# The delta rule's turns placed by a schedule clock among the projections, and its memory handed first to attention's inputs

## The chip, the core and the metric

The kernel runs on one core of a Trainium2 chip. The metric is the device time of one execution in microseconds (us). A core has TensorE (PE in the profile; its weight loads are PEld), VectorE (DVE), ScalarE (ACT), GpSimd (POOL) and SyncE (SP, which here issues nearly all DMAs). Each engine works through its own list of instructions, and semaphores make one wait for another.

## What is computed

One layer of 2048 tokens and width 1024, with two groups of four heads that read the same normalised input:

```python
h = rmsnorm(x, norm_gain)
proj = einsum('btd,dc->btc', h, w_in)          # 4104 columns
dn_q, dn_k, dn_v, dn_z, dn_b, dn_a, df_q, df_k, df_v, df_z = split(proj)
o_dn = gated_deltanet_group(...)   # conv of width 4, SiLU, delta rule with decay, norm(o) * silu(z)
o_df = diff_attention_group(...)   # two causal softmax maps a head, A1 - lam * A2, norm * silu(z)
x = x + einsum('btc,cd->btd', concatenate([o_dn, o_df]), w_out)
```

The delta rule, head by head, is a recurrence over chunks: a triangular system is solved for each chunk, and a state of 128x128 goes from chunk to chunk.

## The kernel before

Matmul inputs are split into a high and a low part of type fp32r, and a product is three matmuls (high by high, high by low, low by high). The kernel is written as generators, each of which gives the hand back (`yield`) after a small piece of work, called a turn or a step here. The order of the program is the order in which the generators are called; the framework then schedules each engine's list from it, by readiness as it reckons it, and `tc.issue_after` keeps what stands in its block behind a given instruction on the same engine.

**Projections** (`feed`, L859 to L888; the generators before it). They come in two halves of 1024 tokens. Each half makes for every head a chunk of delta-rule projections (`dn_chunks`: q, k, v and the gate z, 8 products of 24 matmuls of 512 columns, PE output `pct`), and besides them seven chunks for attention (`rest`): three for q and k (`qk_chunk`, 8 products of 24 matmuls of 256 columns, output `pnat`; the first head's goes ahead of them), two for v (`v_chunk`, likewise 192 matmuls of 256 columns) and two for the gate (`z_chunk`, 96 matmuls of 512 columns, output `pct`). `ORDER` says how many of `rest` go ahead of a head's delta-rule chunk; more go while units of the head before have not yet passed the point where their inputs' buffers come free (`passed` against `ready`). What is left of `rest` follows at the half's end.

**Delta rule** (`gdn`). A unit is one head and 512 tokens; there are 16. `gdn_unit` (from L577) builds the system and inverts it block by block in some 30 turns: transposes `knp`, `qnp`, `vnp`, products `gqp`, `lp`, then rounds of `xq`, `nq`, `tp` and of `xp`, `np`, `tp`, and at the end `rp`, `cp`, `wp`, `ubp`. Two chains work on two units at a time, each in its own PSUM bank (`ua0`, `ua1`). `gdn_scan` (L783) runs the recurrence over a unit's four blocks (`ysp`, `op`), normalises, transposes (`otp`) and stores the result by SP to `mx_d`; the scans of all units come one after another.

**Output projection** (`out_half`, `out_last`). The first half of `w_out` (the delta rule's) is loaded by `load_wout` (L1176): eight DMAs into two raw buffers (`wor`), ACT rounds each to `wo` (L1184), POOL makes the low part (L1185). Then 16 tiles of 128 tokens, each an SP load `mt` of the mixed values and 2 x 12 matmuls `outp` with 5 idle steps after each 12; ACT copies the sum and SP stores it to `part_d`. The second half does the same for attention's values and adds `part_d` and x.

**Attention** (`attention`, L1147) goes through 32 groups of a head and 256 queries, `LOWER` first (the first 1024 tokens), in turns of `scores` (PE `sp`, maximum on DVE `nm`, exponential on ACT `ex`), `values` (PE `wtp`, `oT`) and `epilogue` (`onp`, `aotp`). `load_k` and `load_group` (`k`, `qs`, `azz`) load its inputs by SP, `load_v` its v.

**What sets the order** is `mingle` (L137). It takes one turn of a stream a, then lets as many steps of a stream b follow as `rate` says, and ties these steps behind a's turn `slack` turns back. Before the change it runs twice. First a is the delta rule (the two chains and the scans in rotation, L910 to L920), and b is `behind` (L1278): the projections at 5.25 steps a turn; then, as the projections' memory is closed (`open_early`), attention's first k and q loads, `load_wout(0)`, and the output projection of the first eight tiles, all beside the delta rule's last turns. When the delta rule is done, `open_late` closes its memory and opens attention's; `mingle` runs again with attention as a and the rest of `behind` as b, at 1.0 steps a turn (5.0 near the end).

Of the kernel before, what the change touches and what calls it, by code (L numbers as in the profile page):

```python
# [10 lines left out]
F32 = mybir.dt.float32  # L11
# [5 lines left out]
P = 128  # L17
# [18 lines left out]
ORDER = ((0, 0, 1, 1), (0, 0, 1, 1))  # L36
RATE = 5.25
RATE_T = 5.25
RATE_D = 5.25
SLACK = 4  # L40
# [11 lines left out]
QKB = 5  # L52
RATE_A = 1.0
RATE_B = 1.0
RATE_C = 5.0
# [9 lines left out]
EXB = 14  # L65
WTB = 4

LEVELS = [1, 2, 4, 8, 16, 32, 64]
# [31 lines left out]
def hybrid_kernel(  # L100
# [22 lines left out]

    last = [None]

    class Recorder:


        def matmul(self, *a, **k):
            last[0] = nc.tensor.matmul(*a, **k)  # L130

        def transpose(self, *a, **k):
            last[0] = nc.tensor.transpose(*a, **k)  # L133

    PE = Recorder()

    def mingle(a, b, rate, slack=0, drain=True):  # L137

        credit = 0.0
        steps = [None] * (slack + 1)  # L140
        done = object()
        while a or (b and drain):
# [12 lines left out]
            a = None if r is done else a  # L155
            b = None if q is done else b
        return b

# [418 lines left out]
    def gdn_unit(h, g):  # L577
# [25 lines left out]
        A.activation(AT, df, AF.Exp)  # L603
        yield

# [4 lines left out]
        for i in range(2):  # L610
# [9 lines left out]
            yield  # L620
        V.tensor_scalar(ssn, ssn, 4.0 * EPS, None, op0=ALU.add)
# [20 lines left out]
        PL.affine_select(U, U, pattern=[[0, NCH], [1, P]], compare_op=ALU.is_ge, fill=0.0, base=-1, channel_multiplier=-1)  # L642
        yield
        for j2 in range(2):
# [6 lines left out]
            V.tensor_tensor(AT[:, cs], gq[:, :, 1, :], AT[:, cs], op=ALU.mult)  # L651
            yield

# [39 lines left out]
        def transposed(N):  # L693
# [5 lines left out]
            return TT  # L699

        TT = transposed_packed()
        yield
        for i in PACKED:
# [13 lines left out]
            V.tensor_tensor(X, xp_, lmask[:, off : off + 2 * P], op=ALU.mult)  # L717
            yield
            np_ = flat(ua(gg, "nq")[:, :2, :])
# [3 lines left out]
            if i < PACKED[-1]:  # L723
                for m, r in enumerate(strips):
# [3 lines left out]
                    )  # L728
            yield
            TT = transposed_packed() if i < PACKED[-1] else transposed(N)  # L730
            yield
        for i in WIDE[1:]:
# [13 lines left out]
            V.tensor_tensor(blocks(X), blocks(xp_), odd(lm(i)), op=ALU.mult)  # L746
            yield
# [4 lines left out]
            yield  # L752
            TT = transposed(N)
            yield

# [4 lines left out]
        V.tensor_tensor(R, idb, rp, op=ALU.subtract)  # L760
        yield
        cp = ua(gg, "cp")
# [3 lines left out]
        V.tensor_tensor(NF, f(N), cp, op=ALU.add)  # L766
        yield
# [4 lines left out]
        A.mul(nw, wp_, -1.0)  # L772
        ubp = ua(gg, "ubp")
        for j in range(NCH):
# [5 lines left out]
        solved[0] += 1  # L780
        yield

    def gdn_scan(h, g):  # L783
        if 1:
# [5 lines left out]
            for j in range(NCH):  # L790
                S = state[h]
                ysp = psg.tile([P, 2, P], F32, tag="ysp", name="ysp", bufs=1)
                PE.matmul(ysp[:, 0, :], lhsT=u["nw"][:, j, :], rhs=S, start=True, stop=True)
                yield
                y = gp.tile([P, P], F32, tag="y", name="y", bufs=2)
# [6 lines left out]
                state[h] = S2  # L802
                yield

# [12 lines left out]
            V.tensor_tensor(on, op, bc(fo.unsqueeze(2), S4), op=ALU.mult)  # L817
            yield
            otp = psg.tile(S4, F32, tag="op", name="otp", bufs=2)
# [3 lines left out]
            scanned[0] += 1  # L823
            yield

# [64 lines left out]
    def gdn():  # L890
# [18 lines left out]

        live = [chain(0), chain(1), scans()]  # L910
        while live:
            idle = True
            for c in list(live):
                try:
                    if next(c) is None:
                        idle = False
                        yield
                except StopIteration:
                    live.remove(c)
            if idle and live:  # L920
                yield "wait"


    psa = ap = pso = kp = op_ = None

    def open_early():

        nonlocal pso, kp, op_
        p1.close()
        pso = ctx.enter_context(tc.tile_pool(name="pso", bufs=1, space=PSUM, reuse_waits="tile"))  # L930
        op_ = ctx.enter_context(tc.tile_pool(name="op", bufs=1, reuse_waits="tile"))
        kp = ctx.enter_context(tc.tile_pool(name="kp", bufs=1, reuse_waits="tile"))

    def open_late():
# [3 lines left out]
        ap = ctx.enter_context(tc.tile_pool(name="ap", bufs=2, reuse_waits="tile"))  # L938

    def bank(tag, name, bufs, shape=S4):  # L940
# [235 lines left out]
    def load_wout(half):  # L1176

        wo = {}
        for ch in range(2):
            wo[ch] = hi, lo = [op_.tile([P, KT // 2, G], F32R, tag=f"wo{i}{ch}", name=f"wo{i}{ch}") for i in range(2)]  # L1180
            for k in range(KT // 2):
                raw = op_.tile([P, G], F32, tag="wor", name="wor", bufs=WOR)
# [95 lines left out]
    def behind():  # L1278

        nonlocal cmask  # L1280
        yield from feed()
        pace[0] = RATE_D
        open_early()
        zero = kp.tile([P, P], F32, tag="azz", name="zero", bufs=QSB)
        V.memset(zero, 0.0)
        cmask = kp.tile([P, P], F32R, name="cmask", bufs=1)
        PL.affine_select(cmask, zero, pattern=[[-1, P]], compare_op=ALU.is_ge, fill=NEG, base=0, channel_multiplier=1)
        prefetch(1, 2)
        wo = yield from load_wout(0)
        for tt in range(T // P):  # L1290

            while scanned[0] < (2 * H if tt < 8 else 4 * H - (tt < 12)):
                yield "wait"
            yield from out_half(0, tt, wo)
        wo = yield from load_wout(1)
# [14 lines left out]
        yield from out_last(wo)  # L1310

    cmask = None
    b = mingle(gdn(), behind(), pace, SLACK, drain=False)
    while op_ is None:
        next(b)
# [32 lines left out]
```

## Time and profile before

| | us |
|---|---|
| median of 3 runs | 1719.23 (1713.98 to 1720.64) |
| the profiled execution, its own time | 1721.24 |
| its span from first to last instruction | 1719.5 |
| PE busy | 1592.8 (93%) |
| DVE busy | 1070.1 (62%) |
| ACT busy | 788.0 (46%) |
| POOL busy | 701.7 (41%) |

Shares are of the whole span, over stages that differ: projections and delta rule up to about 1089 us, a stretch in which the delta rule ends and attention starts, and attention with the output projection from about 1165 us on. A busy PE is not a PE at its peak, since matmuls overlap: a matmul's duration in a row is longer than the distance to the next one's start. PEclk is the share of the full clock that PE was granted; there are two levels, 1.2 and 2.4 GHz, so a mean of 0.9 is a stretch with a fifth of its time at the lower one.

### The profile page before, as it was taken

The page shows a single profiled execution, that of the slowest core. Times are in us where ns is not written, and L with a number is a line of the kernel's source. Part 1 is how long each engine was busy: PE and PEld are TensorE (multiplying, and loading weights), DVE is VectorE, ACT ScalarE, POOL GpSimd, SP SyncE. Part 2 cuts the span into 40 slices and gives each one's busy share as a digit, 9 for nine tenths or more (in the row PEclk, how much of TensorE's full clock was granted, in tenths as well). Part 3 has the DMA queues.
Part 4 walks back from the last instruction along what each step waited for, and adds up shares of the span by engine and source line. Part 5 has one row for each costly group of instructions (what it writes and reads, how often), then busy time and mean ns, then how long its engine had stood idle before and what let it go on. Part 6 is the DMA issues. An engine that isn't in the chain of part 4 may idle for free.

```text
span 1719.5 us, 27366 instructions
## 1 busy us (share of the span) xinstructions
PE 1592.8 (93%) x9388; PEld 1377.8 (80%) x9388; DVE 1070.1 (62%) x2435; ACT 788.0 (46%) x2409; POOL 701.7 (41%) x853
## 2 busy tenths in 40 slices
PE   5799999999999799999999999889999989999997
PEld 5688898888987788888888898677877767777876
DVE  4575665755445486557573643337889778888872
ACT  5343344334345343433334333236777656565540
POOL 3356165453242257427345244112334344443333
PEclk8899999999999899999999999989999989999999
DMA  8242234324334452433323232687743283653344
GB/s 165 68 101 54 60 83 94 79 74 76 60 105 104 70 128 57 83 66 82 90 54 104 41 68 87 153 243 201 199 146 116 96 220 111 179 154 103 99 152 161
DMA packets 187032, 188.51 MB, mean 110 GB/s; under 512 B 12243, under 2 KB 142413, under 8 KB 186893
## 3 DMA queue, kind: packets, MB, share of 16 engines
q1 hardware_dynamic: 186556, 185.78, 42.9%
q8 instruction: 74, 1.21, 0.3%
q0 software_dynamic: 336, 0.99, 0.2%
q14 instruction: 66, 0.53, 0.1%
HBM read 124.82 MB, written 61.90 MB: 109 GB/s over the span
## 4 chain that ended last, share of the span: by engine, by line
PE 71%; DVE 10%; DMA 8%; POOL 3%; ACT 3%; issue 3%; SPq 1%; DVEq 0%; POOLq 0%; ACTq 0%
PE pct L130 25%; PE pnat L130 13%; PE outp L130 7%; PE oT L130 6%; PE sp L130 5%; DVE nm L1005 2%; PE wtp L133 2%; DMA wr_fqk<-in_w_in_dram 2%; DVE ex L1059 2%; DMA wor<-in_w_out_dram 1%; PE ysp L130 1%; DMA qs<-qst_d 1%; PE gqp L130 1%; PE op L130 1%; ACT ex L1007 1%
## 5 line engine op out<-in xcount | busy, mean ns | idle before, releaser
L1007 ACT ACTIVATE ex<-sp,nm 128x512 f32<-128x512 f32 (+3 forms) x320 | 198.4, 625 | 100.2 <-DVE nm L1005 83.1
L130 PE MATMUL outp<-wo,mt 128*128 128x512 f32 x720 | 209.2, 422 | 15.5 <-ACT wo L1184 8.0
L1005 DVE TENSOR_REDUCE nm<-sp 128x1 f32<-128x512 f32 (+3 forms) x320 | 186.6, 601 | 27.9 <-PE sp L130 26.1
L130 PE MATMUL sp<-k,qs 128*128 128x512 f32 (+3 forms) x640 | 184.6, 394 | 19.6 <-ACT ex L1007 18.4
L130 PE MATMUL pnat<-wh_fqk,xh 128*128 128x256 f32 (+1 forms) x512 | 155.0, 304 | 27.0 <-ACT xh L334 11.1
L130 PEld LDWEIGHTS outp<-wo,mt 128*128 128x128 f32 x720 | 132.3, 195 | 41.5 <-ACT wo L1184 8.7
L130 PE MATMUL pnat<-wl_fqk,xh 128*128 128x256 f32 (+1 forms) x512 | 151.9, 298 | 1.4 <-POOL wl_fqk L354 1.3
L130 PE MATMUL pnat<-wh_fqk,xl 128*128 128x256 f32 (+1 forms) x512 | 151.9, 298 | 0.0
L130 PEld LDWEIGHTS sp<-k,qs 128*128 128x128 f32 x640 | 108.0, 192 | 48.3 <-ACT ex L1007 35.5
L1055 POOL TENSOR_SCALAR ex<-ex,al 128x512 f32<-128x512 f32 (+3 forms) x140 | 93.7, 685 | 96.5 <-ACT al L1016 89.0
L130 PE MATMUL oT<-wt,v 128*128 128x256 f32 (+1 forms) x576 | 131.6, 372 | 1.4 <-ACT wt L1065 1.4
L545 DVE SCALAR_TENSOR_TENSOR cy<-craw,cc,cy 128x512 f32<-128x512 f32 x144 | 125.0, 869 | 3.0
L130 PEld LDWEIGHTS pnat<-wh_fqk,xh 128*128 128x128 f32 x512 | 102.6, 201 | 29.9 <-ACT wh_fqk L353 11.4
L130 PEld LDWEIGHTS oT<-wt,v 128*128 128x128 f32 x576 | 107.7, 192 | 17.4 <-ACT wt L1065 2.4
L1059 DVE SCALAR_TENSOR_TENSOR ex<-ex,cf 128x512 f32<-128x512 f32 (+3 forms) x160 | 113.2, 751 | 11.7 <-ACT cf L1034 11.3
L130 PEld LDWEIGHTS pnat<-wl_fqk,xh 128*128 128x128 f32 x512 | 102.6, 201 | 2.7 <-POOL wl_fqk L354 2.3
L130 PE MATMUL pct<-xh,wl_dvz 128*128 128x512 f32 x256 | 103.6, 405 | 0.0
L130 PE MATMUL pct<-xl,wh_dvz 128*128 128x512 f32 x256 | 103.5, 404 | 0.0
L130 PE MATMUL pct<-xh,wh_dvz 128*128 128x512 f32 x256 | 103.2, 404 | 0.0
L130 PE MATMUL pct<-xh,wh_dqk 128*128 128x512 f32 x256 | 102.4, 400 | 0.0
L130 PEld LDWEIGHTS pnat<-wh_fqk,xl 128*128 128x128 f32 x512 | 102.0, 200 | 0.2
L130 PE MATMUL pct<-xl,wh_dqk 128*128 128x512 f32 x256 | 101.9, 398 | 0.0
(285 smaller groups left out, 4137.0 us busy)
## 6 DMA issues: line engine op xcount, KB each, us to landing
qs<-qst_d SPq DMA_DIRECT2D x128, 128.0 KB, 3.9
mt<-mx_d SPq DMA_DIRECT2D x48, 256.0 KB, 4.2
k<-kst_d SPq DMA_DIRECT2D x40, 256.0 KB, 5.5
wr_dqk<-in_w_in_dram SPq DMA_DIRECT2D x32, 256.0 KB, 5.0
wr_dvz<-in_w_in_dram SPq DMA_DIRECT2D x32, 256.0 KB, 6.9
qst_d<-qkhl SPq DMA_DIRECT2D x16, 512.0 KB
kst_d<-qkhl SPq DMA_DIRECT2D x16, 512.0 KB, 3.6
part_d<-xr SPq DMA_DIRECT2D x32, 256.0 KB, 3.5
```

What stands on the lines that cost most here:

```text
L130: last[0] = nc.tensor.matmul(*a, **k)
L133: last[0] = nc.tensor.transpose(*a, **k)
L545: V.scalar_tensor_tensor(y, raw[:, j : j + G], convc[:, j, idx : idx + 1], y, op0=ALU.mult, op1=ALU.add)
L1005: V.tensor_reduce(mx, sp[:, :w], axis=AX.X, op=ALU.max, negate=True)
L1007: A.activation(e[:, :w], sp[:, :w], AF.Exp, bias=mx, accum_out=ss[:, m, pi : pi + 1])
L1055: PL.tensor_scalar(e0[:, :w], e0[:, :w], al[:, 0, pi : pi + 1], 1.0, op0=ALU.mult, op1=ALU.mult)
L1059: V.scalar_tensor_tensor(e1[:, :w], e1[:, :w], cf[:, pi : pi + 1], e0[:, :w], op0=ALU.mult, op1=ALU.add)
```

## The change

`mingle` no longer drives the delta rule. A new function, `conduct`, keeps a schedule clock that advances by an estimated time for each matmul issued; every turn of the delta rule now yields a number, after which that stream's next turn is due. A turn is placed when the clock reaches its due time, and until then projections are placed. If the projections have nothing to give ("wait"), the clock jumps to the next due time. The two chains and the scans are three separate streams.

When the delta rule's turns are all placed, `between` runs, mingled with what is left of the projections at up to 12 steps a turn: it closes the delta rule's memory (before: the projections' memory was closed first), opens the pools of k, q and the output weights in its place, issues the first k and q loads and loads the first half of `w_out`. Then the projections are finished, their memory goes to attention's other pools and to the output tiles, and attention starts. All 16 tiles of the first output half now go beside attention, at 1.3 steps a turn.

```diff
-RATE_D = 5.25
+RATE_D = 12.0
-RATE_A = 1.0
-RATE_B = 1.0
+RATE_A = 1.3
+RATE_B = 1.3
+def LAT(us):
+    return 0.4 + 1.4 * us
+    clock = [0.0]
...
+        def matmul(self, out, lhsT, rhs, **k):
+            last[0] = nc.tensor.matmul(out, lhsT=lhsT, rhs=rhs, **k)
+            n = int(np.prod(rhs.shape[1:]))
+            clock[0] += 2 * max(0.11, 0.00084 * n) if rhs.dtype == F32 else max(0.11, 0.00046 * n)
         def transpose(self, *a, **k):
             last[0] = nc.tensor.transpose(*a, **k)
+            clock[0] += 0.11
...
+    def conduct(streams, b):
+        live = [[0.0, i, x] for i, x in enumerate(streams)]
+        steps = [None] * (SLACK + 1)
...
+        while live:
+            x = min(live)
+            if x[0] <= clock[0] or not b:
+                clock[0] = max(clock[0], x[0])
+                last[0] = None
+                r = next(x[2], done)
+                if last[0]:
+                    steps = steps[1:] + [last[0]]
+                if r is done:
+                    live.remove(x)
+                else:
+                    x[0] = clock[0] + (0.3 if r == "wait" else r)
...
+            else:
+                step = steps[0]
+                with tc.issue_after(step.ins) if step else ExitStack():
+                    q = next(b, done)
+                if q == "wait":
+                    clock[0] = x[0]
...
```

The turns' numbers, in the order of a unit: 0.3; `knp` 2.3; `qnp` 2.3; `vnp` 5.0; `gqp` 1.1 twice; `lp` 4.5 (`tp` is now a turn of its own); `tp` 0.5; four rounds of `xq` 0.6, `nq` 1.1, `tp` 0.5 (the last 0.8); two rounds of `xp` 0.6, `np` 0.6, `tp` 0.8; `rp` 0.9; `cp` 0.9; `wp` 0.8 (`ubp` is now a turn of its own); `ubp` 0.9. In a scan: 0.6 after the first product of each of the four blocks, 0.3 after the second (2.5 after the last block), 5.0 ahead of `otp`, 0.3 at the end. Each is written as `yield LAT(...)` in the place of `yield`.

```diff
     def open_early():
-        nonlocal pso, kp, op_
-        p1.close()
-        pso = ...
-        op_ = ...
-        kp = ...
+        nonlocal pso, kp, wop, cmask
+        pg.close()
+        pso, kp, wop = ...  side="right"
+        zero = kp.tile([P, P], F32, tag="azz", name="zero", bufs=QSB)
...
     def open_late():
-        nonlocal psa, ap
-        pg.close()
+        nonlocal psa, ap, op_
+        p1.close()
...
     def behind():
         yield from feed()
-        pace[0] = RATE_D
-        open_early()
...
-        prefetch(1, 2)
-        wo = yield from load_wout(0)
+        fed[0] = True
+        while ap is None:
+            yield "wait"
         for tt in range(T // P):
-            while scanned[0] < (2 * H if tt < 8 else 4 * H - (tt < 12)):
-                yield "wait"
-            yield from out_half(0, tt, wo)
+            yield from out_half(0, tt, first_wo[0])
...
+    def between():
+        open_early()
+        prefetch(1, 2)
+        yield
+        first_wo[0] = yield from load_wout(0)
-    b = mingle(gdn(), behind(), pace, SLACK, drain=False)
-    while op_ is None:
+    b = conduct(gdn(), behind())
+    pace[0] = RATE_D
+    b = mingle(between(), b, pace, SLACK, drain=False)
+    while not fed[0]:
         next(b)
     open_late()
```

`RATE` and `RATE_T` go from 5.25 to 4.0, but `conduct` does not read them.

## Rows read from the trace of the kernel before

**Rows 1.** First line of the page.

```profile
span 1719.5 us, 27366 instructions
```

**Rows 2.** Windows of the stages: length, busy us (instructions) by engine, PEclk, DMA share, GB/s.

```profile
86.00:516.00 430.00, 417.09 (x2660) 370.92 (x2659) 249.82 (x493) 173.32 (x540) 198.58 (x225) 0.99 0.35 79
516.00:602.00 86.00, 73.65 (x489) 66.31 (x488) 44.62 (x103) 39.11 (x97) 21.89 (x21) 0.92 0.45 87
602.00:1089.00 487.00, 472.73 (x2965) 419.37 (x2965) 276.87 (x570) 190.55 (x584) 222.37 (x244) 0.98 0.33 77
1089.00:1165.00 76.00, 61.91 (x321) 51.71 (x321) 26.47 (x72) 24.57 (x70) 14.94 (x13) 0.89 0.91 233
1165.00:1334.00 169.00, 160.09 (x886) 135.19 (x885) 142.55 (x424) 121.88 (x410) 58.33 (x103) 0.99 0.58 162
1334.00:1634.00 300.00, 276.64 (x1414) 224.38 (x1413) 242.43 (x553) 180.67 (x554) 124.39 (x171) 0.98 0.47 137
```

**Rows 3.** Pieces of the chain that ended last: start us, length us, what.

```profile
71.97 11.12 PE pct L130 x48
...
591.80 6.01 PE pnat L130 x48
```

**Rows 4.** Pieces of the same chain between 1080 and 1200 us.

```profile
1085.55 0.37 PE xp L130 x4
...
1113.36 0.63 ACT wo L1184
...
1114.06 1.29 POOL wo L1185
...
1122.23 7.20 DMA wor<-in_w_out_dram
1129.45 0.63 ACT wo L1184
...
1155.54 2.78 PE outp L130 x12
```

**Rows 5.** SP's queue in order of time from 1089 us: start, length, line, DMA.

```profile
1089.62 0.81 SPq L1183 DMA_DIRECT2D wor<-in_w_out_dram  x2
...
1091.01 0.45 SPq L516 DMA_DIRECT2D z_d<-zz  x1
...
1095.36 2.44 SPq L957 DMA_DIRECT2D k<-kst_d  x4
```

**Rows 6.** Windows of tile outp alone: length, busy us of PE, PEld, DVE, ACT.

```profile
1089.00:1150.00 61.00, 23.58 (x71) 14.81 (x72) 0.00 (x0) 2.93 (x5) 0.86 0.91 230
1150.00:1165.00 15.00, 9.44 (x38) 6.55 (x37) 0.00 (x0) 1.76 (x3) 1.00 0.95 247
```

**Rows 7.** PE's groups from 86 to 1089 us: busy, mean ns, idle before, releaser.

```profile
L130 PE MATMUL pnat<-wh_fqk,xh 128*128 128x256 f32 (+1 forms) x448 | 132.8, 298 | 12.2 <-ACT wh_fqk L353 9.9 <-DVE zz L510 1.7 <-ACT qkraw L472 0.6
...
L133 PE MATMUL qktp<-ident,qkraw 128*128 128x128 f32 x116 | 25.8, 309 | 12.6 <-DVE qkraw L482 10.3 <-DVE qkhl L491 1.6
...
L130 PE MATMUL nq<-u_N,identr 128*128 128x256 f32 x62 | 21.4, 345 | 1.4 <-DVE u_X L717 1.3
...
L133 PE MATMUL tp<-identr,u_Nc 128*128 128x128 f32 x63 | 15.9, 253 | 2.2 <-DVE qkss L475 1.5 <-ACT u_Nc L725 0.7
...
L133 PE MATMUL otp<-ident,on 128*128 128x128 f32 x56 | 8.5, 274 | 2.7 <-DVE on L817 2.7
```

**Rows 8.** Timeline from 867 us: one unit's knp and what reads it.

```profile
867.72 0.38 PE L133 MATMUL knp<-ident,kq 128*128 128x128 f32 x2
...
871.85 0.68 DVE L618 TENSOR_TENSOR u_Kg<-knp,ts_eg 128x512 f32<-128x512 f32 x1
...
872.46 0.67 DVE L619 TENSOR_TENSOR kd<-knp,ts_edk 128x512 f32<-128x512 f32 x1
```

**Rows 9.** PE's groups from 1165 to 1634 us, columns as in rows 7.

```profile
L130 PE MATMUL sp<-k,qs 128*128 128x512 f32 (+3 forms) x582 | 168.9, 396 | 19.5 <-ACT ex L1007 18.4
...
L133 PE MATMUL wtp<-ident,ex 128*128 128x128 f32 x493 | 76.9, 279 | 8.2 <-DVE ex L1059 4.0 <-ACT wt L1065 2.6 <-DVE nm L1005 0.7
```

More of the change, by code (lines that the diff above doesn't have):

```diff
@@ L36 @@
 ORDER = ((0, 0, 1, 1), (0, 0, 1, 1))
-RATE = 5.25
-RATE_T = 5.25
-RATE_D = 5.25
+RATE = 4.0
+RATE_T = 4.0
+RATE_D = 12.0
 SLACK = 4
@@ L156, in mingle @@
             b = None if q is done else b
+        return b
+    def conduct(streams, b):
+        live = [[0.0, i, x] for i, x in enumerate(streams)]
+        steps = [None] * (SLACK + 1)
+        done = object()
+        stuck = 0
+        while live:
[10 more added lines that the diff above has]
+                    x[0] = clock[0] + (0.3 if r == "wait" else r)
+                stuck = stuck + 1 if r == "wait" else 0
+            else:
[4 more added lines that the diff above has]
+                    clock[0] = x[0]
+                elif q is done:
+                    b = None
+                else:
+                    stuck = 0
+            assert stuck < 1000, "stuck"
         return b
@@ L603, in gdn_unit @@
         A.activation(AT, df, AF.Exp)
-        yield
+        yield LAT(0.3)
         ssn = t("ssn", "ssn", shape=[P, 2, NCH])
@@ L699, in transposed @@
             return TT
+        yield LAT(4.5)
         TT = transposed_packed()
-        yield
+        yield LAT(0.5)
         for i in PACKED:
@@ L728, in gdn_unit @@
                     )
-            yield
+            yield LAT(1.1)
             TT = transposed_packed() if i < PACKED[-1] else transposed(N)
-            yield
+            yield LAT(0.5 if i < PACKED[-1] else 0.8)
         for i in WIDE[1:]:
@@ L751, in gdn_unit @@
             V.tensor_tensor(No, f(No), blocks(np_), op=ALU.subtract)
-            yield
+            yield LAT(0.6)
             TT = transposed(N)
-            yield
+            yield LAT(0.8)
         rp = ua(gg, "rp")
@@ L760, in gdn_unit @@
         V.tensor_tensor(R, idb, rp, op=ALU.subtract)
-        yield
+        yield LAT(0.9)
         cp = ua(gg, "cp")
@@ L766, in gdn_unit @@
         V.tensor_tensor(NF, f(N), cp, op=ALU.add)
-        yield
+        yield LAT(0.9)
         wp_ = ua(gg, "wp")
@@ L772, in gdn_unit @@
         A.mul(nw, wp_, -1.0)
+        yield LAT(0.8)
         ubp = ua(gg, "ubp")
@@ L780, in gdn_unit @@
         solved[0] += 1
-        yield
+        yield LAT(0.9)
     def gdn_scan(h, g):
@@ L802, in gdn_scan @@
                 state[h] = S2
-                yield
+                yield LAT(0.3 if j < NCH - 1 else 2.5)
             rqs = u["rqs"]
@@ L908, in scans, with open_late @@
                         yield from gdn_scan(h, 2 * hf + gg)
[L910 to L920, printed above, removed]
-                yield "wait"
-    psa = ap = pso = kp = op_ = None
-    def open_early():
-        nonlocal pso, kp, op_
-        p1.close()
[L930 to L934, printed above, removed]
-        nonlocal psa, ap
-        pg.close()
+        return [scans(), chain(0), chain(1)]
+    psa = ap = pso = kp = op_ = wop = None
+    fed = [False]
+    def open_early():
+        nonlocal pso, kp, wop, cmask
+        pg.close()
+        pso = ctx.enter_context(tc.tile_pool(name="pso", bufs=1, space=PSUM, reuse_waits="tile", side="right"))
+        kp = ctx.enter_context(tc.tile_pool(name="kp", bufs=1, reuse_waits="tile", side="right"))
+        wop = ctx.enter_context(tc.tile_pool(name="wop", bufs=1, reuse_waits="tile", side="right"))
+        zero = kp.tile([P, P], F32, tag="azz", name="zero", bufs=QSB)
+        V.memset(zero, 0.0)
+        cmask = kp.tile([P, P], F32R, name="cmask", bufs=1)
+        PL.affine_select(cmask, zero, pattern=[[-1, P]], compare_op=ALU.is_ge, fill=NEG, base=0, channel_multiplier=1)
+    def open_late():
+        nonlocal psa, ap, op_
+        p1.close()
         psa = ctx.enter_context(tc.tile_pool(name="psa", bufs=1, space=PSUM, reuse_waits="tile"))
         ap = ctx.enter_context(tc.tile_pool(name="ap", bufs=2, reuse_waits="tile"))
+        op_ = ctx.enter_context(tc.tile_pool(name="op", bufs=1, reuse_waits="tile"))
     def bank(tag, name, bufs, shape=S4):
@@ L1179, in load_wout @@
         for ch in range(2):
-            wo[ch] = hi, lo = [op_.tile([P, KT // 2, G], F32R, tag=f"wo{i}{ch}", name=f"wo{i}{ch}") for i in range(2)]
+            wo[ch] = hi, lo = [wop.tile([P, KT // 2, G], F32R, tag=f"wo{i}{ch}", name=f"wo{i}{ch}") for i in range(2)]
             for k in range(KT // 2):
-                raw = op_.tile([P, G], F32, tag="wor", name="wor", bufs=WOR)
+                raw = wop.tile([P, G], F32, tag="wor", name="wor", bufs=WOR)
                 SY.dma_start(out=raw, in_=wod[:, half * KT // 2 + k, ch * G : (ch + 1) * G])
```

25 lines of the change are left out of this document (9 added, 16 removed).

## The prediction

> **What bounds the kernel now.** The span is 1719.5 us [rows 1]; the profiled run's own time is 1721.24, 1.7 more, and 2.0 (0.1%) above the median of 1719.23. I sum against 1721.2 and leave the 2 us, which are small beside the range. I read the windows by stage first [rows 2]. PE is busy for 417 of 430 us, 74 of 86, 473 of 487, 62 of 76, 160 of 169 and 277 of 300: it is the bound in every stage, and the question is only where it waits. Its busy time flatters it, however. A run of 48 projection matmuls of 512 columns takes 11.12 us on the chain, 0.232 each, and 48 of 256 columns 6.01, 0.125 each [rows 3], although one of the latter lasts 0.3 us in its group [rows 7]. So I count work by distance from start to start.
>
> The weakest stretch is the junction, 1089 to 1165 us. There PE issues 109 output matmuls [rows 6] at 2.78/12 = 0.232 [rows 4], 25 us, and 321 - 109 = 212 small ones at 0.37/4 = 0.09 [rows 4], 20 us: 45 us of work in 76. **31 us are lost**: 14 as open idle, the rest under a granted clock of 0.89 (a fifth of the stretch at 1.2 GHz) and at the pace of whatever each matmul waits for. DMA is busy for 0.91 of it. The chain says why: the eight loads of the output weights start at 1089.6 [rows 5], when the last projection has freed the memory that they go to, and the last is rounded at 1129.45 + 0.63 [rows 4]. For 40 us the filler that should cover the delta rule's last turns has no weights.
>
> The other waits are spread. From 86 to 1089 us the open idle is 430 - 417 + 86 - 74 + 487 - 473 = 39 us; 12.2 of it lie ahead of q-k projections (a weight load) and 12.6 ahead of `qktp` (waiting for the normalised q and k), both inside the projections' own code [rows 7]. Before the delta rule's thirteen kinds of PE instruction it is 11 us in all; the three largest are 2.7, 2.2 and 1.4 [rows 7]. In attention, 1165 to 1634 us, 32 us are open idle, 19.5 ahead of `sp` and 8.2 ahead of `wtp` [rows 9].
>
> **The change, part by part.** No computation is added or taken away: PE has the same matmuls.
>
> *The junction.* Only the end of the delta rule and the start of attention move. Is there still projection work when `between` begins? By the code's own numbers a unit's 29 waits sum to 32.8 us of latency, so 29 x 0.4 + 1.4 x 32.8 = 57.5 us of due time, and a scan's to 18.7. A unit with its scan issues about 132 PE instructions at 0.09 to 0.11 us, some 13; two units go abreast, so about 75 us pass until both are solved, and then two scans of 23 in a row: 121 us after the last delta-rule chunk. In that time the half has left, by my count (one chunk of `rest` goes ahead of each of heads 1 to 3, because two units pass within some 26 us and a chunk with the turns placed in it takes over 30), two v chunks and two gate chunks: 2 x 192 x 0.125 + 2 x 96 x 0.232 = 93 us, and about 31 us of delta-rule work between them: 124. So **cover and need end nearly together**, and the delta rule's tail is hidden, while the loads that follow have little left to hide behind. SP's list changes: 4 k loads, 8 q loads, 2 gate loads and 8 weight loads come behind the last scan's two stores and ahead of attention's v loads and of the first `mt`; before, they stood among the scans. ACT's 8 copies and POOL's 8 subtractions now stand ahead of attention's first exponentials, which wait behind them, and `sp` waits for the exponentials.
>
> What the junction then costs no row shows. From below it is 0 (all loads land while the last chunk runs: the two chains' own tiles are last used 45 us before the last scan ends, and the framework frees tile by tile and moves DMAs by readiness, as where a store `z_d` of an earlier step stands behind two loads of a later one [rows 5]). From above it is 41 us: the present 40 us of weight loading [rows 5, 4] with nothing beside it. Alone, eight loads through two buffers with 7.2 + 0.63 + 1.29 us a turn [rows 4] are four turns, 36 us, but that landing was taken at a DMA share of 0.91; the `mt` loads and `part_d` stores that made it so now come later. I take 17, nearer the half than either end because about half of the wait can start under the last projections. Gain: 31 - 17 = **14 us**.
>
> *The output tiles beside attention.* The 109 output matmuls, 25 us, move from the junction into attention; that work is conserved and is no gain by itself, since the time it filled is gone as well (it was in the 45). The gain is in what it fills. Attention has some 720 turns; with 1.3 steps a turn for 1.0, the filler of a turn grows by 0.3 x 0.232 = 0.07 us. From below this saves nothing (or costs some: `sp` would be late for DVE, which is busy for 142 of 169 and 242 of 300 us [rows 2]); from above 25 us, if all of it goes into the 32 us of idle. I take **8**: nearer the lower end, since PE keeps the program's order and most turns do not wait. The 9 `mt` loads and 9 `part_d` stores that go with it are hidden (DMA share 0.58 and 0.47 [rows 2]); the 8 ACT copies of `outp` that go with it [rows 6], 5 us, lie in ACT's idle 47 of 169. The second weight load stays where it is, later by a few turns.
>
> *The turns among the projections.* The rotation gave each stream a turn every third time, about 3 x 5.25 steps, 3 us or more; the new dues run from 0.8 (a latency of 0.3) to 7.4 (5.0). Turns that need long get it, short ones lose slack. Between a gain of all 11 us and the loss of the second rival I take a gain of **3**. The 24.8 us ahead of `qktp` and the first q-k projections stay: nothing in `conduct` knows of them. The constants, the mask and the pools' opening move at no cost; they stand beside PE's work, and without that cover they are two small instructions.
>
> Sum: 14 + 8 + 3 = 25; 1721.2 - 25 = **1696 us**. With all terms at their best (31 + 25 + 11) it is 1654.
>
> **The rivals.** *No cover left at the junction.* If a fourth chunk of `rest` goes ahead of a head, or turns run late, projections end some 20 us before the delta rule. Then scans run bare, and the 36 to 41 us of loads follow. The near tie of 121 and 124 us speaks for it, tile-wise freeing against it. The junction costs its 31 again, or up to 41, and attention's 8 are all: 1713 to 1723, say 1716, no measurable change.
>
> *The turns come before their inputs.* This is the slower side. One unit's `knp` transposes end at 868.1 and the last reader of their bank, `kd`, at 873.1 [rows 8]: 5.0 us, because the convolutions' work stands ahead of it on DVE. The new due is 0.4 + 1.4 x 2.3 = 3.6. PE would stand 1.4 us at `qnp`, 16 times: 22 us. Some 450 short turns, late by 0.04 us each, add 18. Without the 3 us gained, 1721.2 - 22 + 40 = 1739. It decides from 22/640 = 0.035 us a turn for the 640 turns. Against it: the framework can let projections pass a turn that it reckons late, up to four turns. Now the open idle is 11/640 = 0.017 us a turn [rows 7], and by that row the sum stands. The Trainium skill, "TensorE: Matmul & The Clock Gate", in its part on what happens when a matmul is issued, says that matmuls stay in program order and only weight loads are pulled ahead; by that rule alone every early turn is paid in full, and the sum comes to this rival's 1739. The trace agrees that PE idles ahead of such turns while projections are in its list.
>
> *The placement does not reach the chip.* Since the framework orders each engine's list by its own reckoning [rows 5], the delta rule's turns may stand much as before, the gain being the order of memory alone: half of the junction's 14, and attention's 8: 1706.
>
> **How the numbers follow.** Forecast 0.50, placement without effect 0.10, no cover 0.16, slower 0.24. About 0.5%, 9 us, is what a measurement of this kernel tells from no change: faster is under 1711, slower over 1728. The first two lie in faster (0.60), the third nearly all in same; of the forecast's and the fourth's edges as much falls in as out: 0.60, 0.16, 0.24. The range: below, 1670 takes in most of the better half (the junction at 5 and attention at 15 give 1721 - 26 - 15 - 8 = 1672); above, 1740 takes in the slower rival's price and leaves out what is dearer. The forecast's own range is 1675 to 1711.
>
> **What would show it.** Right: no stretch of 40 us with a DMA share of 0.9 between the last `pct` and steady `sp`; the weight copies of ACT end before or within 15 us of the last projection; PE's clock at the junction near 1; last `otp` before or with the last `pct`; idle ahead of `sp` in attention under 19 us. Wrong: idle of PE ahead of `qnp`, `nq`, `ysp` that grows from 11 us to 40 (the slower rival), or a bare tail of `ysp` behind the last `pct` and 30 us of idle ahead of the first `sp` (no cover). The same idle of 11 us and dues unchanged in the trace would be the third rival. I would be wrong altogether if attention's stage, which has no new order of its own, changed by more than 25 us.

## The result, and the profile after

The changed kernel takes 1742.62 us (median of 4 runs, 1738.72 to 1747.76), the kernel before 1716.61 beside it (1713.7 to 1720.64): a ratio of 1.0152, with an interval of 1.0112 to 1.0192. It is **slower** by 26 us, outside the predicted range by 2.6 us. The profiled execution's own time is 1745.25, and its span 24.0 us above that of [rows 1]. The first lines of its page:

```profile
span 1743.5 us, 27333 instructions
...
PE 1599.4 (92%) x9388; PEld 1374.8 (79%) x9388; DVE 1068.2 (61%) x2435; ACT 786.9 (45%) x2409; POOL 698.3 (40%) x853
```

DVE, ACT and POOL are busy for as long as before, and PE has the same matmuls, so the 24 us are waiting on PE. The windows of the stages say in which stretches, in the columns of [rows 2]:

```profile
86.00:516.00 430.00, 414.08 (x2702) 366.67 (x2701) 252.18 (x513) 178.16 (x559) 198.92 (x226) 1.00 0.34 79
...
559.00:645.00 86.00, 65.02 (x369) 57.33 (x368) 38.23 (x103) 29.98 (x72) 25.54 (x24) 0.82 0.51 87
645.00:1118.00 473.00, 457.76 (x2916) 403.94 (x2915) 265.61 (x545) 186.47 (x579) 206.70 (x233) 0.99 0.32 73
1118.00:1204.00 86.00, 63.18 (x303) 50.99 (x302) 45.41 (x133) 41.04 (x134) 23.00 (x30) 0.84 0.85 217
...
1334.00:1634.00 300.00, 278.98 (x1422) 226.49 (x1421) 236.64 (x535) 178.70 (x546) 120.52 (x166) 0.99 0.49 147
```

Two stretches are thin: the change of halves (65 us busy of 86, granted clock 0.82; before it was 74 of 86 at 0.92 [rows 2]; in the 80 us from the second half's first `xtp` it is 59 at 0.81 for 68 at 0.91) and the junction (63 of 86 at 0.84). The rest looks much as before, but busy time hides waits here, because it counts matmuls by their length, not by the distance at which they follow each other.

So I tallied **lost time** by distance from start to start, as the prediction did. Each kind of matmul (tile and columns) has a distance to the next start that the quickest fifth of its kind keeps, over all profiles of this study (`pct` and `outp` 0.230 us, `pnat` 0.117, the delta rule's small ones mostly 0.108). What the next matmul starts later than that is lost time, put down to the late matmul. The columns: up to 86 us; among the projections, ahead of the delta rule's turns and ahead of all else; the change of halves (80 us from the second half's first `xtp`); the junction (from the last projection or the last `otp`, whichever is first, to 50 us into attention); the rest of attention and the bare end. In us:

| profile | to 86 | turns | others | halves | junction | attention, end | sum |
|---|---|---|---|---|---|---|---|
| before | 34 | 33 | 64 | 21 | 38 | 87 | 278 |
| after | 33 | 71 | 42 | 34 | 36 | 86 | 303 |
| e1 | 32 | 52 | 53 | 22 | 55 | 93 | 309 |
| e2 | 33 | 71 | 43 | 31 | 34 | 119 | 332 |
| e3 | 32 | 71 | 41 | 30 | 34 | 104 | 313 |
| e4 | 33 | 70 | 44 | 21 | 34 | 91 | 293 |
| e5 | 33 | 44 | 46 | 17 | 44 | 99 | 282 |
| e6 | 33 | 80 | 43 | 34 | 17 | 99 | 308 |
| e7 | 34 | 55 | 56 | 31 | 50 | 130 | 356 |
| e8 | 35 | 75 | 46 | 20 | 21 | 95 | 293 |
| e9 | 34 | 48 | 43 | 16 | 35 | 95 | 270 |
| e10 | 35 | 43 | 44 | 17 | 32 | 103 | 275 |
| e11 | 33 | 34 | 65 | 22 | 30 | 102 | 286 |
| e12 | 33 | 48 | 46 | 17 | 34 | 99 | 278 |

(Rows add up to their sum within 2 us, by rounding; the sums differ as the spans do within about 2.) Of after against before: **turns +38, others -22, halves +13, junction -2, attention -1**. The column of the turns does not hold the same matmuls in every row, since a turn in the change of halves or behind the last projection counts in that column: it has 2082 of the delta rule's 2112 in after, 1784 in before, 1872 in e5, 1770 in e1. At before's loss for each, after's would have lost 39, so some 32 of the 38 us are dearer turns and 6 are more of them.

**The turns.** PE's groups from 86 to 1131 us, as in [rows 7]:

```profile
L137 PE MATMUL pnat<-wh_fqk,xh 128*128 128x256 f32 (+1 forms) x448 | 133.5, 299 | 13.6 <-ACT wh_fqk L396 11.6 <-ACT qkraw L515 1.3 <-DVE zz L553 0.4
L137 PE MATMUL ysp<-state,nw 128*128 128x128 f32 x128 | 26.1, 286 | 7.7 <-DVE state L844 7.5
L142 PE MATMUL qktp<-ident,qkraw 128*128 128x128 f32 x116 | 22.1, 277 | 3.0 <-DVE qkhl L534 1.6 <-DVE qkraw L525 1.3
L137 PE MATMUL nq<-u_N,identr 128*128 128x256 f32 x64 | 21.5, 337 | 3.3 <-DVE u_X L761 3.1
L137 PE MATMUL xq<-u_N,u_Lc 128*128 128x256 f32 x64 | 21.0, 329 | 3.1 <-ACT u_TT L733 2.9
L137 PE MATMUL wp<-u_NF,u_Kg 128*128 128x128 f32 x128 | 19.0, 295 | 3.4 <-DVE u_NF L810 3.4
L142 PE MATMUL tp<-identr,u_Nc 128*128 128x128 f32 x64 | 15.7, 245 | 5.9 <-ACT u_Nc L769 5.8
L142 PE MATMUL xtp<-ident,xt 128*128 128x128 f32 x64 | 11.4, 302 | 7.2 <-DVE xl L378 6.1 <-DVE xt L282 0.7 <-ACT qkraw L515 0.2
L142 PE MATMUL qnp<-ident,kq 128*128 128x128 f32 x64 | 9.7, 272 | 0.0
L142 PE MATMUL otp<-ident,on 128*128 128x128 f32 x60 | 9.1, 275 | 0.0
```

`ysp` waits 7.7 us for the `state` that the turn before it has DVE write, `tp` 5.9 for `u_Nc`, `wp` 3.4, `nq` 3.3, `xq` 3.1: all are turns with short dues (0.8 to 1.9 us). In the kernel before, from 86 to 1089 us, beside `nq` and `tp` of [rows 7]:

```profile
L130 PE MATMUL ysp<-state,nw 128*128 128x128 f32 x112 | 22.3, 281 | 0.9 <-DVE state L799 0.8
L130 PE MATMUL xq<-u_N,u_Lc 128*128 128x256 f32 x63 | 21.4, 339 | 0.5 <-ACT u_TT L690 0.4
L130 PE MATMUL wp<-u_NF,u_Kg 128*128 128x128 f32 x112 | 14.5, 276 | 0.3 <-DVE u_NF L766 0.3
```

`qnp` and `otp`, with numbers of 2.3 and 5.0 (dues of 3.6 and 7.4 us), wait for nothing. The other way about, `qktp`, which waited 12.6 us [rows 7], waits 3.0; by starts that is some 17 us, most of the "others" column.

**The change of halves.** The waits that PE has there, by who ends them (times, longest), from 559 to 645 us:

```profile
PE pnat L137 <- ACT wh_fqk L396: 11.6, 1, 11.6
ACT wh_fqk L396 <- DMA wr_fqk<-in_w_in_dram: 11.5, 1, 11.5
...
PE xtp L142 <- DVE xl L378: 6.1, 4, 2.2
```

The weight load is not new: `pnat` waited 9.9 us for it before [rows 7]. New is that nothing of the delta rule is left beside it and the transposes: its first half is through at about 574 us, and in the 80 us only 20 of its matmuls are issued, against 166 before.

**The junction.** SP's queue and PE's timeline:

```profile
1126.68 0.39 SPq L1003 DMA_DIRECT2D v<-v_d  x1
1127.12 1.25 SPq L1263 DMA_DIRECT2D mt<-mx_d  x2
...
1138.94 0.67 SPq L879 DMA_DIRECT2D mx_d<-mxh  x1
1140.28 0.33 SPq L879 DMA_DIRECT2D mx_d<-mxl  x1
1140.70 2.44 SPq L997 DMA_DIRECT2D k<-kst_d  x4
1143.24 2.57 SPq L1012 DMA_DIRECT2D qs<-qst_d  x4
...
1150.44 0.91 SPq L1223 DMA_DIRECT2D wor<-in_w_out_dram  x2
...
1174.68 0.33 SPq L1223 DMA_DIRECT2D wor<-in_w_out_dram  x1
```

```profile
1130.52 0.40 PE L137 MATMUL pct<-xh,wl_fz 128*128 128x512 f32 x1
...
1136.34 1.08 PE L142 MATMUL otp<-ident,on 128*128 128x128 f32 x4 [4.05 <-DVE on L862]
1150.55 0.66 PE L137 MATMUL sp<-k,qs 128*128 128x128 f32 x2 [13.12 <-DMA qs<-qst_d]
```

The last projection ends at 1130.9 us and the delta rule 6 us later: cover and need do end together. But the k and q loads are issued only behind the last scan's two stores, and PE stands 13.1 us for `qs`. The weight loads follow, one by one, up to 1174.7. Loads of v and the first `mt`, which the prediction put behind them, were issued from 1126.7 on, ahead of the last scan's stores.

### The profile page after: what moved, and what is told of

The parts are those of the page before. It is cut to its first block, busy times and chain, and to the rows that moved or that the text cites. A ratio compares the mean times of both kernels' runs of the same rounds, so it can differ in the third digit from the quotient of the medians.

```text
span 1743.5 us, 27333 instructions
## 1 busy us (share of the span) xinstructions
PE 1599.4 (92%) x9388; PEld 1374.8 (79%) x9388; DVE 1068.2 (61%) x2435; ACT 786.9 (45%) x2409; POOL 698.3 (40%) x853
## 5 line engine op out<-in xcount | busy, mean ns | idle before, releaser
L137 PE MATMUL outp<-wo,mt 128*128 128x512 f32 x720 | 203.8, 416 | 3.0 <-DVE xr L1276 1.4
L137 PE MATMUL pnat<-wh_fqk,xh 128*128 128x256 f32 (+1 forms) x512 | 155.0, 304 | 27.9 <-ACT wh_fqk L396 12.6
L1099 DVE SCALAR_TENSOR_TENSOR ex<-ex,cf 128x512 f32<-128x512 f32 (+3 forms) x160 | 116.9, 773 | 25.1 <-ACT cf L1074 10.9
L588 DVE SCALAR_TENSOR_TENSOR cy<-craw,cc,cy 128x512 f32<-128x512 f32 x144 | 121.3, 843 | 2.5
L137 PE MATMUL pct<-xh,wl_dqk 128*128 128x512 f32 x256 | 103.1, 406 | 0.0
```

The lines of the kernel that those rows point to most:

```text
L137: last[0] = nc.tensor.matmul(out, lhsT=lhsT, rhs=rhs, **k)
L588: V.scalar_tensor_tensor(y, raw[:, j : j + G], convc[:, j, idx : idx + 1], y, op0=ALU.mult, op1=ALU.add)
L1099: V.scalar_tensor_tensor(e1[:, :w], e1[:, :w], cf[:, pi : pi + 1], e0[:, :w], op0=ALU.mult, op1=ALU.add)
```

## The experiments

Each lists its edit of the changed kernel, unless it says otherwise.

**e1: the rotation with the new order of memory.** The three streams in rotation again, in the place of `conduct`:

```diff
-    b = conduct(gdn(), behind())
+    b = mingle(rotate([chain0, chain1, scans_]), behind(), pace, SLACK, drain=False)
```

with `RATE` and `RATE_T` at 5.25.

> The delta rule's turns go by rotation at 5.25 steps a turn as before the change; memory order, the weight load between, and attention's rate 1.3 stay as changed. Theory A (the early placing empties the change of halves: nothing of the delta rule is left to run beside its loads): the stretch around the second half's first projections goes back from 21 us of open PE idle in 86 us to about 12, as before the change, and the last projection from 1131 us back to about 1090. But the delta rule's tail of 60 us then has no filler at all and the loads come behind it, so the whole takes 1745 to 1765. Rival B (the turns come before their inputs, spread over all of the projections): the last projection comes back to about 1090 as well, but the gain is spread evenly, not at the change of halves. Rival C (the junction alone is at fault): the last projection stays near 1131.

1753.38 us, ratio to before 1.0191 [1.0162, 1.022]. The change of halves and the tail behind the last projection:

```profile
559.00:645.00 86.00, 74.63 (x514) 68.30 (x513) 52.74 (x130) 33.52 (x92) 29.48 (x31) 0.94 0.49 93
1092.00:1151.00 59.00, 33.57 (x204) 28.07 (x203) 20.05 (x51) 11.61 (x39) 6.07 (x6) 0.79 0.50 129
```

The change of halves is covered again (22 us lost for 34), and the last projection is back at 1092.7 us. What was gained there goes at the junction (55 us): the delta rule's last 45 us run with nothing beside them, because the new memory order lets no output tile in. So the new memory order needs the dues. The turns lose 52 us, between before's 33 and after's 71, although the rotation is before's. Two of the groups, from 86 to 1092 us:

```profile
L137 PE MATMUL xq<-u_N,u_Lc 128*128 128x256 f32 x61 | 21.3, 364 | 3.5 <-ACT u_TT L733 3.5
L142 PE MATMUL tp<-identr,u_Nc 128*128 128x128 f32 x61 | 15.3, 262 | 8.2 <-ACT u_Nc L769 8.1
```

`tp` and `xq` wait at least as long as in after, without any dues. e1 keeps the change's finer turns (the first `tp` and `ubp` apart), which were not tried alone.

**e2: the dues with the old order of memory.** `open_early`, `open_late`, `behind` and the rates as before; `conduct` stays.

> The turns are placed by their dues as in the change, but the projections' memory is closed first, the output weights and the first output tiles stand behind the projections, and attention's rate is 1.0, as before. Theory A: the change of halves still idles for 20 us, the last projection still ends near 1130. Junction: the delta rule ends with the projections, so the 40 us of weight loads have next to no delta-rule work beside them, 10 to 25 us worse than the kernel before: 1745 to 1765. If the new order of memory is what costs (rival C), this comes out at 1720 or less.

1778.26 us, 1.0343 [1.0308, 1.0379], the worst but one. The table's columns up to the junction are within 3 us of after's. The 33 us that it is over after, by the ratios, come later: with the projections used up at 1128 us there is no tail for the tiles to fill, and at one step a turn attention is over long before they are (119 us lost in attention and end). The new order of memory is therefore not what loses the time before attention.

**e3: one step a turn.** `RATE_A` and `RATE_B` at 1.0.

> The change with attention's rate at 1.0 for 1.3, nothing else. Theory D (the higher rate pays in the middle of attention, where open idle ahead of sp fell, and is given back at the end): middle 8 to 12 us slower, end 8 to 10 us faster, the whole within 5 us of the change's 1743. If the rate pays outright as I forecast: 8 us slower, 1751. If the rate costs: 1735.

1760.3 us, 1.025 [1.0215, 1.0284], 17 us over after by the ratios. The last group of attention starts its epilogue at 1657 us, 70 earlier than in after, and from there PE has output tiles alone:

```profile
1657.00:1752.30 95.30, 73.27 (x269) 55.26 (x268) 17.44 (x28) 2.47 (x8) 24.95 (x23) 0.88 0.62 196
```

So with all 16 tiles beside attention the rate of 1.3 pays against 1.0. I had expected next to no difference, and that fell.

**e4: the last head of the first half stretched.**

```diff
-                    yield from gdn_unit(h, 2 * hf + gg)
+                    for r in gdn_unit(h, 2 * hf + gg):
+                        yield r * (2.0 if hf == 0 and h == 3 else 1.0)
```

> The change, with all dues of the two units of the first half's last head doubled, so that their turns reach over the change of halves; nothing else. Theory A: open PE idle there falls from 21 us to about 12 and the granted clock rises from 0.82 to above 0.9: 10 to 17 us are won, 1726 to 1733. Rival B: only the stretched units' own waits, an eighth of all, go away: 1 to 3 us, 1740 to 1742. If the second half's first units are held up by it, some of the gain is lost again there.

1735.48 us, 1.0097 [1.0072, 1.0122]: some 9 us better than after by the ratios. The stretch is covered:

```profile
559.00:645.00 86.00, 75.70 (x492) 68.89 (x493) 54.84 (x128) 30.89 (x78) 32.48 (x33) 0.92 0.50 96
```

The weight load still stands open, in PE's groups from 86 to 1118 us:

```profile
L137 PE MATMUL pnat<-wh_fqk,xh 128*128 128x256 f32 (+1 forms) x448 | 132.0, 296 | 14.6 <-ACT wh_fqk L396 11.2 <-ACT qkraw L515 1.8 <-DVE zz L553 1.4
```

Lost at the change are 21 us, as before; turns stay at 70. The bare change of halves is thus a cause of its own, worth 13 us in its stretch and 9 in the end.

**e5: longer short dues.** The numbers after `xq`, `nq`, `tp`, `rp`, `cp` and a scan's second product raised to what the waits suggest (the line of `LAT(0.9)` twice):

```diff
-            yield LAT(0.6)
+            yield LAT(1.0)
-            yield LAT(1.1)
+            yield LAT(2.0)
-            yield LAT(0.5 if i < PACKED[-1] else 0.8)
+            yield LAT(1.0 if i < PACKED[-1] else 0.8)
-        yield LAT(0.9)
+        yield LAT(1.5)
-                yield LAT(0.3 if j < NCH - 1 else 2.5)
+                yield LAT(1.0 if j < NCH - 1 else 2.5)
```

> The change with the dues raised where PE was found waiting for a turn's input: the state in a scan (a latency of 0.3 to 1.0), nq (1.1 to 2.0), the packed tp (0.5 to 1.0), the packed xq (0.6 to 1.0), rp and cp (0.9 to 1.5); nothing else. Theory B (turns placed before their inputs): the open idle ahead of the delta rule's PE groups falls from 29 us towards 15, the last projection ends 10 to 15 us sooner. A unit and two scans get some 20 us longer by their dues, so the delta rule ends behind the projections and the junction gets worse by about as much: the whole within 8 us of the change's 1743. If the 29 us have another cause (a slower clock, DVE's load), the idle stays within 4 us of 29.

1721.54 us over 10 runs, 1.0018 [1.0002, 1.0033]: 23 us of the 26 are back. PE's groups from 86 to 1083 us, and the window:

```profile
L137 PE MATMUL pnat<-wh_fqk,xh 128*128 128x256 f32 (+1 forms) x448 | 130.7, 294 | 2.6 <-DVE zz L553 1.1 <-ACT qkraw L515 1.1
L137 PE MATMUL ysp<-state,nw 128*128 128x128 f32 x116 | 22.5, 276 | 0.9 <-DVE state L844 0.9
L137 PE MATMUL nq<-u_N,identr 128*128 128x256 f32 x64 | 21.3, 334 | 1.5 <-DVE u_X L761 1.5
L137 PE MATMUL xq<-u_N,u_Lc 128*128 128x256 f32 x64 | 21.0, 327 | 3.7 <-ACT u_TT L733 3.7
L142 PE MATMUL tp<-identr,u_Nc 128*128 128x128 f32 x64 | 15.6, 244 | 7.1 <-ACT u_Nc L769 6.6
L142 PE MATMUL xtp<-ident,xt 128*128 128x128 f32 x64 | 9.7, 276 | 0.5 <-DVE xl L378 0.5
```

```profile
559.00:645.00 86.00, 81.14 (x491) 70.98 (x491) 56.52 (x133) 33.55 (x87) 32.88 (x37) 0.98 0.55 107
```

Turns lose 27 us less (44 for 71), some 20 of it for the same number of matmuls; their idle column falls from 29.1 to 20.3 us. `ysp` hardly waits any more and `nq` half as long, while `xq` and `tp`, whose dues were raised too, wait no less than in after. And the delta rule now lasts to 592 us in the first half: the change of halves loses 17 us less. Both gains come from the longer dues, as nothing else was changed. At the change, some 11 of the 17 are the wait for the weight load, which is gone (`pnat` 2.6 us in all, 13.6 in after); e4, whose delta rule lasts longer still, has it. What covers it here was not tried. Given back are 8 us at the junction, where the delta rule now ends 22 us behind the last projection, and 13 in attention.

**e6: the last head of the second half hurried.** `gdn_unit` and `gdn_scan` of its units with dues x 0.7 (in e4's manner, `0.7 if hf == 1 and h == 3`), so that loads go while projections are left.

> The change with all dues of the last head of the second half, units and scans, at 0.7 of their size; nothing else. Theory C (k, q and the output weights can load only once the last scan has freed the delta rule's memory, and then no projection is left beside them): the delta rule ends some 25 us ahead of the last projection, those loads run beside projections, and 15 to 25 us are won: 1718 to 1728, with the hurried turns' own waits some 3 us on the other side. Rival: the junction is bound by what comes with the projections' memory (v, the first output tiles, attention's own buffers): under 6 us won, 1737 or more.

1752.17 us, 1.0193 [1.0175, 1.0211], some 7 worse than after by the ratios. SP's queue and PE's timeline:

```profile
1126.23 0.32 SPq L879 DMA_DIRECT2D mx_d<-mxl  x1
1126.64 2.68 SPq L999 DMA_DIRECT2D k<-kst_d  x4
```

```profile
1142.01 0.40 PE L137 MATMUL pct<-xh,wl_fz 128*128 128x512 f32 x1
1142.25 0.33 PE L137 MATMUL sp<-k,qs 128*128 128x128 f32 x2
```

The loads follow the last scan's stores again, now 16 us ahead of the last projection, and `sp` follows the last `pct` with no gap. The junction loses 17 us in place of 36: that is the 13 us wait with its surroundings, and the mechanism is shown. But shorter dues cost 9 us more at the turns, and attention loses 13 more.

**e7: all dues longer, old memory.** `LAT(us)` = 0.8 + 2.0 * us on e2's kernel.

> The dues of the change, but 0.8 + 2.0 us for 0.4 + 1.4 us of latency, with the order of memory and the rates of the kernel before. The delta rule then lags behind the projections about as far as under rotation and has the output tiles as filler. Theories A and B together: waits ahead of the delta rule's turns near or under the 11 us of the kernel before, change of halves covered, junction as before: 1705 to 1725. If placing by dues is worse than rotation in itself: 1730 or more.

1802.49 us, 1.0484 [1.0468, 1.05]. The projections are back at 1102 us, but the delta rule is not through before 1229. Turns lose 55 us, more than in e5 (44), which lengthens only the short ones. With the old order of memory and one step a turn, longer for all is the wrong remedy.

**e8: e4 and e6 together.**

> The stretched last head of the first half (dues doubled, as in the run before) and the hurried last head of the second half (dues at 0.7) together, the rest as changed. If the two causes add: 8 us and 15 to 25 us off 1743, 1710 to 1720, level with the kernel before or faster. If they are one and the same (only where the delta rule ends against the projections), no more than the better of the two alone.

1734.25 us, 1.0081 [1.0061, 1.0101], no better than e4. Halves (20) and junction (21) are both mended, 29 us less than after; turns take 4 of it, others 4 and attention 9.

**e9: e5 and e6 together.**

> The longer short dues (1721) and, on top, the last head's dues at 0.7, so that the delta rule ends about with the projections instead of 22 us behind them; the rest as changed. If what is left of the loss sits at the junction (a bare tail of the delta rule, then k, q and weight loads): the first scores start at 1100 to 1108 instead of 1118, and 8 to 18 us are won, 1704 to 1714, faster than the kernel before. If hurrying only turns the tail into waits among the projections, as with the change's own dues: within 5 us of 1721.

1715.92 us over 12 runs, 1.0001 [0.9983, 1.002]: level with the kernel before. The profiled span, 1711.1 us, is 8.4 under [rows 1], but the median is not. Here the hurried head did not hide the loads: the delta rule now ends at 1097.7 us, behind the last projection at 1090.2, and PE waits 13.7 us for `qs`.

**e10: e5's dues, the old memory, rates 1.3.**

> The longer short dues with the order of memory of the kernel before (projections' memory closed first, weight loads and the first output tiles behind the projections) and attention's rate 1.3. If the new order of memory is what the junction loses by (k and q wait for the last scan), this beats the longer dues with the new order: the delta rule ends near 1105 with k and q loaded beside it, the first scores start at 1110 to 1125 with some output tiles done, 1700 to 1715. If the 40 us of weight loads need the delta rule's long tail as cover, as with the change's own dues in the old order: 1735 to 1750.

1718.51 us, 1.0018 [0.9998, 1.0038]: with these dues either order of memory comes within 0.2% of the kernel before.

**e11: the kernel before with rates 1.3.**

```diff
-RATE_A = 1.0
-RATE_B = 1.0
+RATE_A = 1.3
+RATE_B = 1.3
```

> The kernel before with attention's rate at 1.3 for 1.0; nothing else. By my forecast's term, more filler a turn fills waits ahead of the scores: 5 to 8 us faster, 1709 to 1712. Against it: the filler runs out sooner and the end of attention stands bare: equal or up to 10 us slower, 1717 to 1727.

1727.66 us, 1.0066 [1.004, 1.0091]. The rate alone costs 11 us here, where 72 of the first half's 384 output matmuls, 3 of the 16 tiles and not eight, run ahead of the first `sp`. From 1634 us to the end, 92.5 us, where before has 85.5:

```profile
1634.00:1726.50 92.50, 77.01 (x351) 61.80 (x349) 45.97 (x95) 24.56 (x72) 28.54 (x33) 0.92 0.41 132
```

In the table the loss lies in attention (102 for 87); the other columns are before's, but for the junction, 8 less.

**e12: e9 with rates 1.2.**

> The longer short dues, the last head's dues at 0.7, and attention's rate at 1.2 for 1.3. Attention from its first scores to the end took 600 us in the profiled run at 1.3. If the rate is too high (filler spent before the last heads, as in the kernel before at 1.3, which lost 11 us): 590 to 595, the whole 1706 to 1711, faster than the kernel before. If it is too low already (output tiles left over behind attention, as at 1.0): 5 to 10 us slower, 1721 to 1726.

1720.04 us, 1.0014 [0.9993, 1.0036]: no gain from a rate between. No kernel of the study is measurably faster than the one before.

## Why the prediction was wrong

The forecast of 1696 failed; the second rival, turns before their inputs at 1739, is the nearest to what happened, some 4 us dearer. That its time comes so near is in part luck: 22 us of its price stood at a turn that cost nothing, and the change of halves (13 us lost) and `qktp` (some 17 won), which it did not have, about cancel.

*The turns.* The step "I take a gain of **3**" is the one that failed most: it is a loss of 38, some 32 of it for the same number of matmuls. The rival's price was 40, of which 22 at `qnp` and 18 for short turns late by 0.04 us. `qnp` waits 0.0 us; nearly all is at short turns, on the rival's own 640 turns 0.05 to 0.06 us each, above the 0.035 from which it said it decides. I leaned on [rows 7], where the turns wait 0.017 us each, but that row was taken under a rotation that gave each stream some 3 us, and the dues of 0.8 to 1.9 us had no row behind them. The argument against it, that the framework lets projections pass a late turn, did not hold off the loss. The Trainium skill, "TensorE: Matmul & The Clock Gate", Part 2 on issuing a matmul, says that matmuls stay in program order; by that rule every early turn is paid for, and the trace agrees: `ysp` stands 7.7 us for `state` with projections still to do. e5 shows that the dues are the cause of the waits at `ysp`, `wp` and `nq`, which fall from 7.7, 3.4 and 3.3 us to 0.9, 2.0 and 1.5 with longer ones. It does not show it for `tp` and `xq`: with longer dues they wait 7.1 and 3.7 us, under the rotation (e1) 8.2 and 3.5, in the kernel before 2.2 and 0.5. With `xp`, they lose some 26 us by the tally in after, 27 in e1 and in e5, and 12 in the kernel before, so 12 to 14 of the 38 are not explained by the dues. The finer turns, which e1 and e5 share with after, may be it; this is argued, not shown.

*What I called untouched.* "The 24.8 us ahead of `qktp` and the first q-k projections stay" was wrong on both sides. `qktp` fell from 12.6 us to 3.0, a gain that I had not looked for. Why was not tried; all runs with dues have it, e11 (the kernel before in this respect) has not, and e1, rotation with finer turns, stands between (6.1). And the change of halves, where I saw only the weight load, lost 13 us more: a delta rule that runs ahead is through before it, and leaves it bare. No term and no rival had this. I had counted how long the delta rule takes at the end of the second half, and not at the end of the first. e4 shows it.

*The junction.* The count held: 124 us of cover against 121 of need, and the ends lie 6 us apart. The gain of 14 did not come; it is 2. The step that failed is "about half of the wait can start under the last projections". Nothing did: in after, e6 and e9 the k loads are issued 0.4 us behind the start of the last scan's `mxl` store, wherever the projections are. With both ends together the k and q loads, the rounding and the weight loads then run one after the other: 13.1 us until the first `sp`, and 49 until the last weights are rounded (about 1180 us). The upper end I kept, loads with nothing beside them, was the nearer one. e6 moves that point 16 us ahead of the last projection, and 19 us come back; that such a place for the loads pays at the junction is shown, though that run lost more elsewhere (9 at the turns, 13 in attention). Whether it is the freed memory or SP's own order that holds the k loads behind the store was not told apart. The order of the program alone is not it: the v and `mt` loads, which come later in the program, were issued ahead of the store. They go to the projections' memory, so this leans to the freed memory, but does not show it.

*Attention.* "I take **8**" measured 1 by the table. The open idle did fall, as forecast: 14.6 us ahead of `sp` and 5.4 ahead of `wtp` between 1204 and 1634 us, for 19.5 and 8.2 [rows 9] in a stretch that is 39 us longer. It is lost again in the pace and at the end. **What stays open** is attention's own spread: e4, e5, e6, e8 and e9 leave its code and rates as in after, and it loses 91 to 99 us in them, and 86 in after. The framework puts their lists together in different orders, but which order costs what I can't show. Part of why e8 gains nothing over e4 lies there (4 us; its turns and others take 7), and so does why e5 is not ahead of the kernel before: up to attention it loses 184 us against 190, and from there 99 against 87.

*The checks.* Of those named as right, only the idle ahead of `sp` and the last `otp` near the last `pct` (6 us behind it) came true; the DMA share at the junction (0.95 for the 49 us from 1131 us on), the clock (0.76 there) and the weight copies (49 us behind the last projection) did not. Of those named as wrong, the turns' idle rose from 11.2 us to 29.1, at `ysp`, `tp`, `wp`, `nq` and `xq`, not at `qnp` and not to the 40 that were named.

## What to carry to other kernels

A schedule clock is worth what its latencies are worth: measure each turn's from the last matmul of one turn to the first of the next under the load that it will run in, and give the short ones slack first. Here early turns were paid for in order, and longer short dues took some 20 us off them, while 8 us were given back at the junction, where the delta rule then ended behind its cover (e5). Look at each turn again after that, since some waits (`tp`, `xq`) did not fall with longer dues. A stream that runs faster than its cover also leaves bare whatever stood beside its end (here a weight load and transposes in the middle, loads at the junction), so count what covers what at every border, not only at the last. Before moving loads behind a last user, look at what is left to run beside them from that point on.

## What the hardware showed that I had not expected

A small wait repeated is worth as much as a large one: no turn's group waited more than 7.7 us in all, and the turns together lost 38 us more than before. About half of that is not in the idle column (29.1 us, up 18 from 11.2) but in matmuls that overlap less, seen only from start to start. At the change of halves the granted clock was 0.82, a third and more of the stretch at the lower level, and PE stood for 2.2 us, then 11.6, then up to 1.6 at a time. With the delta rule beside it, it was 0.92 in e4, which still stands 11.2 us for the weight load, and 0.98 in e5, which does not.
